# The last up projection of a two-layer encoder by Strassen's scheme, with the gated chunks kept in DRAM

## The chip, the cores and the metric

The kernel runs on one core of one Trainium2 chip. Its time is the device time of one execution in microseconds (us), the median of several runs. TensorE does the matrix products, VectorE (DVE in the profile) and ScalarE (ACT) everything that is done per element, GpSimd (POOL) a few small operations, and SyncE's queue (SP) starts the transfers.

## What is computed

The input is 1024 tokens of 1024 numbers. Two layers follow one another; each has a token mixer (sparse attention in layer 0, retention in layer 1) and then a gated feed-forward part with a short causal convolution. The change is in the feed-forward part of the last layer:

```python
def conv_ffn(h, w_up, conv_w, conv_b, w_down):
    seq = h.shape[1]
    u = h @ w_up                                   # (1024, 1024) @ (1024, 5632)
    up = jnp.pad(u, ((0, 0), (CONV_W - 1, 0), (0, 0)))
    u = sum(up[:, j:j + seq] * conv_w[j] for j in range(CONV_W)) + conv_b
    a, b = u[..., :D_FF], u[..., D_FF:]            # D_FF = 2816 = 22 chunks of 128
    return (jax.nn.silu(a) * b) @ w_down

x = x + conv_ffn(rms_norm(x, norm_ffn_g[i]), f_w_up[i], f_conv_w[i], f_conv_b[i], f_w_down[i])
```

## The kernel before

Channels lie on the 128 partitions and tokens along the rows; the 1024 tokens are two halves of 512, and `x[0]`, `x[1]` hold the running sum of each half as 8 chunks of 128 channels. Every product of two float32 matrices is made of three: each operand is split into a high part `hi` (a ScalarE copy to a narrower format) and a rest `lo` (a VectorE subtraction), and `mm3` (L134 to L136) adds hi times hi, hi times lo and lo times hi in one bank of PSUM, the accumulator memory. There are 8 banks of 128 x 512 numbers.

Weights come through a queue. `wprep` loads one block of 128 x 1024 into `wraw` (2 buffers), splits it into `whi` (L98) and `wlo` (L100; 3 buffers each), and `weight` keeps two blocks ahead of the one in use.

The last stage is `ffn` in mode `FULL`, over both halves at once. For each of the 22 chunks `c` it makes four projections (`proj_T`, 24 matmuls each: chunk `c` and chunk `22 + c` of the weights, for each half); `conv` takes each bank, multiplies it by the tokens' 1/rms (L552), and applies the three taps (L556 to L558; the last two columns of the first half are kept in `halo` for the second); then SiLU (L576), the product with the other side (L578) and the split into `ghf`, `glf` (L580, L581). After every fourth chunk the down projection of that group follows, 8 blocks of weights for both halves, each result added to `x` (L593). The normalised input `hh`, `hl` of a half is `x` times a gain, split (L145, L146); 1/rms is applied afterwards. For the first half this is done inside the second half's retention (`early` in `retention`), for the second half behind it.

The order in which each engine's instructions stand is made by a planner when the program is built, from the order of the code and what each instruction waits for. On the chip every engine keeps its order: an instruction that waits holds up all that stand behind it on its engine, the issue of transfers on SP's queue too.

## Time and profile before

| | |
|---|---|
| median of 3 runs | 2853.04 us (2852.39 to 2853.21) |
| span of the profiled execution, first to last instruction | 2850.1 us |
| TensorE busy | 2755.8 us, 97% of the span |
| VectorE busy | 1823.4 us, 64% |
| ScalarE busy | 1049.9 us, 37% |
| last stage (up and down projection of layer 1) | about from 2112 to the end |

The span leaves out what lies before the first and after the last instruction. Busy time counts an instruction from start to end, so matmuls that overlap in the pipeline are better counted by the distance of their starts.

### The profile page before, as it was taken

What the parts mean: (1) busy time and instruction counts of PE and PEld (TensorE: products, weight loads), DVE (VectorE), ACT (ScalarE), POOL (GpSimd) and SP (SyncE); (2) the same over time, 40 slices, a digit from 0 to 9 for tenths busy, and PEclk for the clock granted to TensorE, in tenths of its full rate; (3) what the DMA queues carried; (4) which work ended last, traced back from release to release, by engine and by line L of the source; (5) the groups of instructions that cost most, each with busy time, mean ns of one, the idle gap of its engine ahead of it and who ended that gap; (6) DMA issues with size and microseconds to landing.
All of it is one profiled execution on the core that took longest, in us unless ns stands there. A gap on an engine that the chain in (4) does not pass through costs nothing.

```text
span 2850.1 us, 32404 instructions
## 1 busy us (share of the span) xinstructions
PE 2755.8 (97%) x12416; PEld 2263.7 (79%) x12416; DVE 1823.4 (64%) x3180; ACT 1049.9 (37%) x1588; POOL 379.1 (13%) x247
## 2 busy tenths in 40 slices
PE   8978998998999999999999999999999999999999
PEld 6756786776787888888888888888888888888887
DVE  5798899997685454455766764444556564656464
ACT  6437433332473333334433443233343232323231
POOL 2554334344430000000000000000000000000000
PEclk9988999999999999999999999999999999999999
DMA  5220123222211222232233232222221111111112
GB/s 193 76 87 32 60 74 94 70 96 74 82 38 67 82 96 74 81 104 74 91 102 96 91 102 97 82 75 95 87 69 45 52 41 56 37 60 34 63 37 90
DMA packets 72763, 217.76 MB, mean 76 GB/s; under 512 B 8224, under 2 KB 10656, under 8 KB 72608
## 3 DMA queue, kind: packets, MB, share of 16 engines
q1 hardware_dynamic: 72608, 215.70, 23.2%
q8 instruction: 97, 1.59, 0.2%
q14 instruction: 58, 0.48, 0.1%
HBM read 205.71 MB, written 6.29 MB: 74 GB/s over the span
## 4 chain that ended last, share of the span: by engine, by line
PE 74%; DVE 11%; issue 1%; ACT 1%; POOL 0%; DMA 0%; POOLq 0%; ACTq 0%; DVEq 0%
PE bank L134 24%; PE bank L136 24%; PE bank L135 24%; DVE scratch L417 4%; DVE t L558 2%; DVE t L557 1%; DVE t L552 1%; PE bank L526 1%; DVE gl L581 1%; DVE x L593 0%; PE bank L759 0%; POOL wlo L100 0%; DVE tkb L427 0%; DVE t L578 0%; ACT hh L145 0%
## 5 line engine op out<-in xcount | busy, mean ns | idle before, releaser
L134 PE MATMUL bank<-hh,whi 128*128 128x512 f32 (+2 forms) x1888 | 738.2, 391 | 16.9 <-ACT hh L145 10.6
L136 PE MATMUL bank<-hh,wlo 128*128 128x512 f32 (+2 forms) x1888 | 736.5, 390 | 10.4 <-POOL wlo L100 10.4
L135 PE MATMUL bank<-hl,whi 128*128 128x512 f32 (+2 forms) x1888 | 735.7, 390 | 3.5 <-DVE hl L146 3.4
L98 ACT ACTIVATE whi<-wraw 128x1024 fp32r<-128x1024 f32 (+4 forms) x416 | 400.0, 962 | 887.9 <-PE bank L135 607.3
L100 DVE TENSOR_TENSOR wlo<-wraw,whi 128x1024 fp32r<-128x1024 f32 (+4 forms) x319 | 350.9, 1101 | 306.8 <-ACT whi L98 303.5
L134 PEld LDWEIGHTS bank<-hh,whi 128*128 128x128 f32 (+1 forms) x1888 | 356.3, 189 | 93.8 <-ACT hh L145 12.3
L136 PEld LDWEIGHTS bank<-hh,wlo 128*128 128x128 f32 (+1 forms) x1888 | 356.1, 189 | 90.3 <-POOL wlo L100 15.1
L135 PEld LDWEIGHTS bank<-hl,whi 128*128 128x128 f32 (+1 forms) x1888 | 356.1, 189 | 79.1 <-DVE hl L146 4.3
L100 POOL TENSOR_TENSOR wlo<-wraw,whi 128x1024 fp32r<-128x1024 f32 (+2 forms) x97 | 219.8, 2268 | 308.9 <-ACT whi L98 293.4
L552 DVE TENSOR_TENSOR t<-bank,rbc 128x512 f32<-128x512 f32 x176 | 120.9, 688 | 169.7 <-PE bank L136 168.4
L556 ACT ACTIVATE t<-t,cols 128x512 f32<-128x512 f32 x176 | 142.5, 813 | 229.8 <-DVE t L552 228.9
L593 DVE TENSOR_TENSOR x<-x,bank 128x512 f32<-128x512 f32 x160 | 109.2, 685 | 181.8 <-PE bank L136 181.4
L135 PE MATMUL bank<-wlo,hh 128*128 128x512 f32 x512 | 199.3, 389 | 0.0
L136 PE MATMUL bank<-whi,hl 128*128 128x512 f32 x512 | 199.2, 389 | 0.0
L134 PE MATMUL bank<-whi,hh 128*128 128x512 f32 x512 | 198.8, 390 | 0.0
L417 DVE TENSOR_SCALAR_CACHE_REDUCE scratch<-sc,tkt 128x640 f16<-128x640 f32 (+1 forms) x192 | 180.5, 940 | 1.9
L558 DVE SCALAR_TENSOR_TENSOR t<-t,cols,t 128x510 f32<-128x510 f32 x176 | 155.9, 886 | 3.8
L136 PE MATMUL bank<-gh,wlo 128*128 128x512 f32 x352 | 139.9, 399 | 14.3 <-POOL wlo L100 14.0
L557 DVE SCALAR_TENSOR_TENSOR t<-t,cols,t 128x511 f32<-128x511 f32 x176 | 142.1, 807 | 11.4 <-ACT t L556 8.6
L134 PE MATMUL bank<-gh,whi 128*128 128x512 f32 x352 | 138.7, 396 | 5.6 <-ACT whi L98 5.6
L135 PE MATMUL bank<-gl,whi 128*128 128x512 f32 x352 | 138.6, 394 | 0.0
L135 PE MATMUL bank<-glf,whi 128*128 128x512 f32 x352 | 136.8, 389 | 0.0
(213 smaller groups left out, 4189.7 us busy)
## 6 DMA issues: line engine op xcount, KB each, us to landing
wraw<-in_wf_up SPq DMA_DIRECT2D x132, 512.0 KB, 3.2
wraw<-in_wb_vg SPq DMA_DIRECT2D x64, 512.0 KB, 3.2
wraw<-in_wf_dn SPq DMA_DIRECT2D x48, 384.0 KB, 3.1
wraw<-in_wb_qk SPq DMA_DIRECT2D x32, 512.0 KB, 3.2
wraw<-in_wb_out SPq DMA_DIRECT2D x32, 512.0 KB, 3.2
wraw<-in_wf_dn SPq DMA_DIRECT2D x56, 256.0 KB, 2.7
wraw<-in_wa_in SPq DMA_DIRECT2D x26, 512.0 KB, 3.4
x<-in_xT SPq DMA_DIRECT2D x16, 512.0 KB, 7.3
```

The lines of the kernel that those rows point to most:

```text
L98: nc.scalar.activation(hi[:, :n], raw[:, :n], AF.Copy)
L100: eng.tensor_tensor(lo[:, :n], raw[:, :n], hi[:, :n].bitcast(F32), ALU.subtract)
L134: mm(ps, ah, bh, start=first, stop=False)
L135: mm(ps, ah, bl, start=False, stop=False)
L136: mm(ps, al, bh, start=False, stop=last)
L417: V.tensor_scalar(scratch[:, 0, :Ls[b]], scs[b], of(b), None, op0=op, op1=ALU.add, accum_out=cnt[:, b:b + 1])
L526: nc.tensor.transpose(pt[:, i * 128:(i + 1) * 128], lg[:, i, j * 128:(j + 1) * 128], self.ident)
L552: nc.vector.tensor_tensor(pn, ps, rbc, ALU.mult)
L556: nc.scalar.activation(u, ps, AF.Identity, bias=w(3), scale=w(2))
L557: nc.vector.scalar_tensor_tensor(u[:, 1:], ps[:, :511], w(1), u[:, 1:], op0=ALU.mult, op1=ALU.add)
L558: nc.vector.scalar_tensor_tensor(u[:, 2:], ps[:, :510], w(0), u[:, 2:], op0=ALU.mult, op1=ALU.add)
L593: nc.vector.tensor_tensor(x[:, m], x[:, m], ps, ALU.add)
```

## The change

Up to the second half's retention both programs issue the same instructions in the same order. Then the last `ffn` is replaced by `ffn_whole`. It takes the product of two blocks of weight outputs (chunk `c`, chunk `22 + c`) by two halves of the input channels with two halves of the channels by two halves of the tokens, a product of 2 by 2 blocks, with 7 block products for 8 (`product`, 12 matmuls each). In exchange there are sums of weight blocks (`t3`, `a21`, `a11`, `a12` in `prep_b`), sums of input blocks made once (`T1` to `T4`), and sums of results (the `add` calls behind the products). Inputs are now normalised in place beforehand (`normaliser`), so `x` is first written to DRAM (`xd`) and read back at the end. The results of both halves lie side by side (`ca`, `cb`, 1024 wide), so the convolution runs once over 1024 columns. SiLU of one side (`ud[0]`) and the other side (`ud[1]`) are written to DRAM. When all 22 chunks are through, a separate loop reads them, multiplies and splits them (`gate`) and makes the down projection in four groups instead of six. The first block products of the first `PRE` = 4 chunks (`first`: those that need only the first half of the tokens) are issued ahead, the first of them inside the retention.

```diff
...
 HALF = ([(0, 6), (6, 6), (12, 6), (18, 4)], 8, 2)
-FULL = ([(0, 4), (4, 4), (8, 4), (12, 4), (16, 4), (20, 2)], 5, 1)
+DOWN = [(0, 6), (6, 6), (12, 6), (18, 4)]
+PRE = 4
...
-    def retention(self, half, x, early):
+    def retention(self, half, x, then=None, early=lambda: None):
...
                 early()
+            if n in (1, 3) and then:
+                next(then)
             for j in range(4):
...
                 nxt = qk_proj(n + 1)
+            elif then:
+                next(then)
             y = self.ogp.tile([128, 2, 4, 512], F32R, tag="og", name="y")
...
                         self.square_sum(x, m)
+                        nc.sync.dma_start(self.xd[half][m], x[:, m])
+    def split(self, hi, lo, raw):
+        return (self.nc.scalar.activation(hi, raw, AF.Copy),
+                self.nc.vector.tensor_tensor(lo, raw, hi.bitcast(F32), ALU.subtract))
+    def normaliser(self, x, gc, half):
+        rbc = self.tp.tile([128, 512], F32, tag="rbc", bufs=1, name="rbc")
+        self.nc.scalar.activation(rbc, self.bcast(self.tok[half][1], range(4)), AF.Copy)
+        def chunk(k):
+            self.nc.vector.scalar_tensor_tensor(x[:, k], x[:, k], self.col(gc + k), rbc, op0=ALU.mult, op1=ALU.mult)
+        return chunk
...
+    def product(self, ps, w, t, first, last):
+        for k in range(4):
+            a, b = w[0][:, k * 128:(k + 1) * 128], w[1][:, k * 128:(k + 1) * 128]
+            for i, (u, v) in enumerate(((a, t[:, 0, k]), (a, t[:, 1, k]), (b, t[:, 0, k]))):
+                self.nc.tensor.matmul(ps, u, v, start=first and k + i == 0, stop=k == 3 and i == 2,
+                                      skip_group_check=not (first and last))
+    def ffn_whole(self, l, x):
+        nc = self.nc
+        add = lambda o, a, b, op=ALU.add: nc.vector.tensor_tensor(o, a, b, op)
+        x0, x1 = x
...
+        def prep_a(c):
+            raw = load(c)
+            return raw, halves(raw)
+        def prep_b(c, raw):
+            rb = load(NFF + c)
+            a11, a12, a21, a22 = raw[:, :512], raw[:, 512:], rb[:, :512], rb[:, 512:]
+            t3 = s3.tile([128, 512], F32, tag="t3", name="t3")
+            add(t3, a11, a21, ALU.subtract)
+            add(a21, a21, a22)
+            s1, a22 = halves(rb)
+            add(a11, rb[:, :512], a11, ALU.subtract)
+            add(a12, a12, a11, ALU.subtract)
+            s2, s4 = halves(raw)
+            return s1, s2, halves(t3, s3, 512, "3")[0], s4, a22
+        def first(wa, keep=None):
+            a, e = self.bank(), self.bank()
+            self.product(a, wa[0], B11, True, False)
+            p1 = self.tmp()
+            nc.scalar.activation(p1, a, AF.Copy)
+            self.product(e, wa[1], B21, True, True)
+            if keep is None:
+                keep = self.tmp()
+            add(keep, e, p1)
+            return a, keep
+        chunk = self.normaliser(x0, gc, 0)
+        for k in range(8):
+            chunk(k)
+        yield
+        B11, B21 = [self.hp.tile([128, 2, 4, 512], F32R, tag="h", name=n) for n in ("B11", "B21")]
+        for t, o in ((B11, 0), (B21, 4)):
+            for k in (0, 2):
+                self.split(two(t, 0, k), two(t, 1, k), two(x0, o + k))
+        wa = [prep_a(0)]
+        yield
+        pre = [first(wa[0][1])]
+        tt, s3 = yield
+        T = lambda name: tt.tile([128, 2, 4, 512], F32R, tag="T", name=name)
+        wa += [prep_a(c) for c in range(1, PRE)]
+        pre.append(first(wa[1][1]))
+        self.mean_square(1)
+        pre.append(first(wa[2][1]))
+        chunk = self.normaliser(x1, gc, 1)
+        pre += [first(w) for _, w in wa[3:]]
+        nxt = prep_b(0, wa[0][0])
+        T1, T2, T4, B22, T3 = [T(n) for n in ("T1", "T2", "T4", "B22", "T3")]
+        for k in (0, 2):
+            chunk(k)
+            chunk(k + 1)
+            add(two(x0, k), two(x1, k), two(x0, k), ALU.subtract)
+            self.split(two(T1, 0, k), two(T1, 1, k), two(x0, k))
+        for k in range(4):
+            chunk(4 + k)
+            t2 = self.tmp()
+            add(t2, x1[:, 4 + k], x0[:, k], ALU.subtract)
+            self.split(T2[:, 0, k], T2[:, 1, k], t2)
+            add(x0[:, 4 + k], x0[:, 4 + k], t2, ALU.subtract)
+        for k in (0, 2):
+            self.split(two(T4, 0, k), two(T4, 1, k), two(x0, 4 + k))
+        for k in (0, 2):
+            self.split(two(B22, 0, k), two(B22, 1, k), two(x1, 4 + k))
+        for k in (0, 2):
+            add(two(x1, k), two(x1, 4 + k), two(x1, k), ALU.subtract)
+            self.split(two(T3, 0, k), two(T3, 1, k), two(x1, k))
+        cu = [self.xp.tile([128, 4, 1024], F32, tag="x", name="cu") for _ in range(2)]
+        def conv(ct, u, c):
+            w = lambda j: self.col(C_CONV + (l * 44 + c) * 4 + j)
+            nc.scalar.activation(u, ct, AF.Identity, bias=w(3), scale=w(2))
+            nc.vector.scalar_tensor_tensor(u[:, 1:], ct[:, :1023], w(1), u[:, 1:], op0=ALU.mult, op1=ALU.add)
+            nc.vector.scalar_tensor_tensor(u[:, 2:], ct[:, :1022], w(0), u[:, 2:], op0=ALU.mult, op1=ALU.add)
+        for c in range(NFF):
+            s1, s2, s3_, s4, a22 = nxt
+            ca, cb, ua, ub = (cu[c % 2][:, i] for i in range(4))
+            if pre:
+                a, c11 = pre.pop(0)
+                nc.scalar.activation(ca[:, :512], c11, AF.Copy)
+            else:
+                a, _ = first(wn, ca[:, :512])
+            d = self.bank()
+            self.product(d, s1, T1, True, False)
+            p5 = self.tmp()
+            nc.scalar.activation(p5, d, AF.Copy)
+            self.product(a, s2, T2, False, False)
+            u2 = self.tmp()
+            nc.scalar.activation(u2, a, AF.Copy)
+            f = self.bank()
+            self.product(f, a22, T4, True, True)
+            p4 = self.tmp()
+            nc.scalar.activation(p4, f, AF.Copy)
+            self.product(d, s4, B22, False, True)
+            add(ca[:, 512:], d, u2)
+            self.product(a, s3_, T3, False, True)
+            add(cb[:, :512], a, p4)
+            add(cb[:, 512:], a, p5)
+            if c + 1 < NFF:
+                raw, wn = prep_a(c + 1) if c + 1 >= PRE else (load(c + 1), None)
+                nxt = prep_b(c + 1, raw)
+            conv(ca, ua, c)
+            nc.scalar.activation(ua, ua, AF.Silu)
+            nc.sync.dma_start(self.ud[0][c], ua)
+            conv(cb, ub, NFF + c)
+            nc.sync.dma_start(self.ud[1][c], ub)
+        todo = [(g0, n, m) for g0, n in DOWN for m in range(8)]
+        ready = []
+        def dn(i):
...
+        buf = self.hp.tile([128, 4, 1024], F32, tag="h", name="gin")
+        gates = {}
+        def gate(c):
+            ga, gb = buf[:, c % 2 * 2], buf[:, c % 2 * 2 + 1]
+            nc.sync.dma_start(ga, self.ud[0][c])
+            nc.sync.dma_start(gb, self.ud[1][c])
+            add(ga, ga, gb, ALU.mult)
+            if c % 2 == 0:
+                p, tag = (self.hp, "h") if c in (0, 12) else (tt, "T")
+                self.gt = p.tile([128, 2, 2, 1024], F32R, tag=tag, name="g")
+            g = self.gt[:, c % 2]
+            self.split(g[:, 0], g[:, 1], ga)
+            gates[c] = g
+        dn(0)
+        gate(0)
+        dn(1)
+        for c in range(1, DOWN[0][1]):
+            gate(c)
+        y = [self.xp.tile([128, 8, 512], F32, tag="x", name="xo") for _ in range(2)]
+        for m in range(8):
+            for h in range(2):
+                nc.sync.dma_start(y[h][:, m], self.xd[h][m])
+        for i, (g0, n, m) in enumerate(todo):
+            if i + 2 < len(todo):
+                dn(i + 2)
+            if m == 2 and g0 + n < NFF:
+                ahead = list(range(g0 + n, min(g0 + n + DOWN[0][1], NFF)))
+            if m >= 2 and g0 + n < NFF and ahead:
+                gate(ahead.pop(0))
+            hi, lo = ready[i]
+            for h in range(2):
+                ps = self.bank()
+                for k in range(n):
+                    g = gates[g0 + k]
+                    sl = slice(h * 512, (h + 1) * 512)
+                    self.mm3(ps, hi[:, k * 128:(k + 1) * 128], lo[:, k * 128:(k + 1) * 128], g[:, 0, sl], g[:, 1, sl],
+                             k == 0, k == n - 1)
+                add(y[h][:, m], y[h][:, m], ps)
+                if g0 + n == NFF:
+                    nc.sync.dma_start(self.out[m * 128:(m + 1) * 128, h * H:(h + 1) * H], y[h][:, m])
     def run(self):
...
         self.plan_weights([("inproj", 0), ("inproj", 1), ("outproj", 0), ("ffn", (0, HALF, True)), ("outproj", 1),
-                           ("ret", 0), ("ffn", (0, HALF, False)), ("ret", 1), ("ffn", (1, FULL, False))])
+                           ("ret", 0), ("ffn", (0, HALF, False)), ("ret", 1)])
...
-            self.ogp = pool("og", 2)
+            inner = es.enter_context(ExitStack())
+            self.ogp = inner.enter_context(tc.tile_pool(name="og", bufs=2, reuse_waits="tile"))
...
+            self.xd = [[dp.tile([128, 512], F32, name=f"xd{h}_{m}") for m in range(8)] for h in range(2)]
+            self.ud = [[dp.tile([128, 1024], F32, name=f"ud{i}_{c}") for c in range(NFF)] for i in range(2)]
...
                 self.later(1, lambda: self.mean_square(1))
-                self.retention(0, x[0], lambda: parts.append(self.ffn_part(0, 1, x[1])))
+                self.retention(0, x[0], None, lambda: parts.append(self.ffn_part(0, 1, x[1])))
...
                 self.later(1, lambda: self.mean_square(1))
-                self.retention(1, x[1], lambda: parts.append(self.ffn_part(1, 0, x[0])))
-            with tc.tile_pool(name="ring", bufs=1, reuse_waits="tile") as rp:
-                og = (self.ogp, "og")
-                self.later(2, lambda: self.mean_square(1))
-                parts.append(self.ffn_part(1, 1, x[1], (og, og), rp, lag=4))
-                R = FULL[1]
-                gh = rp.tile([128, R, 2, 512], F32R, name="ghf")
-                gl = rp.tile([128, R, 2, 512], F32R, name="glf")
-                self.ffn(1, FULL, parts, lambda c, i: (gh[:, c % R, i], gl[:, c % R, i]), last=True)
+                last = self.ffn_whole(1, x)
+                self.retention(1, x[1], last)
+            inner.close()
+            with tc.tile_pool(name="T", bufs=5, reuse_waits="tile") as tt, \
+                    tc.tile_pool(name="s3", bufs=1, reuse_waits="tile") as s3:
+                for _ in iter(lambda: last.send((tt, s3)), None):
+                    pass
...
```

Three places show how the order moves. In `t2_...`, `bank_...` and the like the number tells buffers apart.

The first place is VectorE where the last stage begins. Before, it splits the second half's input (`hl`) and goes straight to the first chunk's convolution:

```order
L146 SCALAR_TENSOR_TENSOR hl_16435<-x_7351,cols_84,hh_16434 128x512 x7
L100 TENSOR_TENSOR wlo_16457<-wraw_16455,whi_16456 128x1024
L185 TENSOR_TENSOR acc_16291<-acc_16291,t2_16427 128x512
L146 SCALAR_TENSOR_TENSOR hl_16435<-x_7351,cols_84,hh_16434 128x512
L552 TENSOR_TENSOR t2_16588<-bank_16467,rbc_16151 128x512
L561 COPY halo_91<-t2_16588 128x2
L557 SCALAR_TENSOR_TENSOR t2_16590<-t2_16588,cols_84,t2_16590 128x511
L558 SCALAR_TENSOR_TENSOR t2_16590<-t2_16588,cols_84,t2_16590 128x510
L194 TENSOR_SCALAR msq_16528<-bank_16523 128x4
L100 TENSOR_TENSOR wlo_16463<-wraw_16461,whi_16462 128x1024
```

Now the eight chunks are first normalised in place (L795); then come the sums and splits of the input blocks (L821 and L787 on `x`, `t2`, `T1` to `T4`, `B22`), among those of the weights (`wraw`) and one sum of a result (`bank`), before any convolution:

```order
L795 SCALAR_TENSOR_TENSOR x_7411<-x_7411,cols_84,rbc_16631 128x512 x8
L821 TENSOR_TENSOR x_2809<-x_7411,x_2809 128x1024
L821 TENSOR_TENSOR t3_16818<-wraw_16814,wraw_16816 128x512
L821 TENSOR_TENSOR x_2809<-x_7411,x_2809 128x1024
L821 TENSOR_TENSOR t2_16666<-bank_16639,t2_16652 128x512
L821 TENSOR_TENSOR t2_16703<-x_7411,x_2809 128x512
L821 TENSOR_TENSOR t2_16709<-x_7411,x_2809 128x512
L821 TENSOR_TENSOR x_7411<-x_7411 128x1024
L821 TENSOR_TENSOR wraw_16816<-wraw_16816 128x512
L787 TENSOR_TENSOR T1_16687<-x_2809,T1_16687 128x1024
L821 TENSOR_TENSOR x_7411<-x_7411 128x1024
L821 TENSOR_TENSOR t2_16715<-x_7411,x_2809 128x512
```

These are the first 12 of 31 rows, 39 instructions in all, down to the split of the second chunk's weights; the convolution begins two rows later.

The second place is VectorE in the middle of the up projection. Before, it works on one chunk half by half, in pieces of 512 columns:

```order
L552 TENSOR_TENSOR t2_16888<-bank_16788,rbc_16151 128x512
L561 COPY halo_91<-t2_16888 128x2
L581 TENSOR_TENSOR glf_16454<-t2_16767,ghf_16453 128x512
L557 SCALAR_TENSOR_TENSOR t2_16890<-t2_16888,cols_84,t2_16890 128x511
L558 SCALAR_TENSOR_TENSOR t2_16890<-t2_16888,cols_84,t2_16890 128x510
L100 TENSOR_TENSOR wlo_16784<-wraw_16782,whi_16783 128x1024
L552 TENSOR_TENSOR t2_16896<-bank_16838,rbc_16151 128x512
L561 COPY halo_91<-t2_16896 128x2
L552 TENSOR_TENSOR t2_16906<-bank_16813,rbc_16452 128x512
L557 SCALAR_TENSOR_TENSOR t2_16898<-t2_16896,cols_84,t2_16898 128x511
```

Now one chunk is 17 instructions; these are 12 of them (L911 and L912 are the convolution, L821 on `bank` takes a result out of PSUM, L787 is a split); two sums of results, a split of 512 and two pieces of convolution make up the rest:

```order
L821 TENSOR_TENSOR t3_17664<-wraw_17656,wraw_17662 128x512
L911 SCALAR_TENSOR_TENSOR cu_16740<-cu_16740,cols_84 128x1023
L821 TENSOR_TENSOR wraw_17662<-wraw_17662 128x512
L821 TENSOR_TENSOR cu_16741<-bank_17557,t2_17570 128x512
L912 SCALAR_TENSOR_TENSOR cu_16740<-cu_16740,cols_84 128x1022
L787 TENSOR_TENSOR wlo_17659<-wraw_17656,whi_17658 128x1024
L821 TENSOR_TENSOR wraw_17656<-wraw_17662,wraw_17656 128x512
L821 TENSOR_TENSOR wraw_17656<-wraw_17656 128x512
L787 TENSOR_TENSOR wlo_17668<-wraw_17662,whi_17667 128x1024
L821 TENSOR_TENSOR cu_16741<-bank_17585,t2_17612 128x512
L787 TENSOR_TENSOR wlo_17674<-wraw_17656,whi_17673 128x1024
L911 SCALAR_TENSOR_TENSOR cu_16741<-cu_16741,cols_84 128x1023
```

The weights that are summed and split here are those of the next chunk, between the results of this one.

The third place is TensorE where the down projection begins. Before, a group of it stood directly behind a chunk's up projection:

```order
L135 MATMUL bank_17163<-hl_16435,whi_16933 128x512
L136 MATMUL bank_17163<-hh_16434,wlo_16934 128x512
L134 MATMUL bank_17232<-ghf_16453,whi_17077 128x512
L135 MATMUL bank_17232<-glf_16454,whi_17077 128x512
L136 MATMUL bank_17232<-ghf_16453,wlo_17078 128x512
L134 MATMUL bank_17232<-ghf_16453,whi_17077 128x512
```

Now it is behind the last chunk; `g_19551` holds the gated chunks 0 and 1, `g_19568` chunks 2 and 3, and six banks stand open at once, so that each gated chunk is used for three blocks of weights before the next one is wanted:

```order
L137 MATMUL bank_19729<-g_19551,whi_19607 128x512
L138 MATMUL bank_19729<-g_19551,whi_19607 128x512
L139 MATMUL bank_19729<-g_19551,wlo_19608 128x512
L137 MATMUL bank_19611<-g_19568,whi_19544 128x512
L137 MATMUL bank_19631<-g_19568,whi_19544 128x512
L137 MATMUL bank_19657<-g_19568,whi_19556 128x512
L137 MATMUL bank_19677<-g_19568,whi_19556 128x512
L137 MATMUL bank_19709<-g_19568,whi_19607 128x512
L137 MATMUL bank_19729<-g_19551,whi_19607 128x512
```

## Rows read from the trace of the kernel before

**Rows 1.** the page's busy times: us, share of the span, instructions

```profile
PE 2755.8 (97%) x12416; PEld 2263.7 (79%) x12416; DVE 1823.4 (64%) x3180; ACT 1049.9 (37%) x1588; POOL 379.1 (13%) x247
```

**Rows 2.** busy time of each engine in a stretch of the last stage

```profile
core 0: us, PE busy (x) PEld busy (x) DVE busy (x) ACT busy (x) POOL busy (x), PEclk, DMA share, GB/s
2200.00:2300.00 100.00, 100.00 (x443) 82.84 (x442) 50.47 (x82) 24.52 (x33) 0.00 (x0) 1.00 0.16 51
```

**Rows 3.** waits of TensorE from 2050 to the end: total us, times, longest

```profile
PE bank L759 <- DVE sg L734: 1.1, 1, 1.1
PE bank L134 <- ACT y L145: 0.5, 1, 0.5
```

**Rows 4.** timeline of TensorE: start us, us, what; 25 matmuls apart

```profile
2079.94 0.39 PE L134 MATMUL bank<-whi,hh 128*128 128x512 f32 x1
...
2085.61 0.39 PE L135 MATMUL bank<-wlo,hh 128*128 128x512 f32 x1
```

**Rows 5.** groups by line and shape, 2100 to the end: busy us, mean ns

```profile
L134 PE MATMUL bank<-hh,whi 128*128 128x512 f32 x704 | 274.1, 389 | 0.0
...
L134 PE MATMUL bank<-ghf,whi 128*128 128x512 f32 x352 | 136.3, 389 | 0.0
...
L556 ACT ACTIVATE t<-t,cols 128x512 f32<-128x512 f32 x88 | 71.2, 815 | 161.4 <-DVE t L552 161.4
...
L558 DVE SCALAR_TENSOR_TENSOR t<-t,cols,t 128x510 f32<-128x510 f32 x88 | 65.8, 748 | 2.1
L557 DVE SCALAR_TENSOR_TENSOR t<-t,cols,t 128x511 f32<-128x511 f32 x88 | 65.8, 748 | 8.9 <-ACT t L556 6.1
L593 DVE TENSOR_TENSOR x<-x,bank 128x512 f32<-128x512 f32 x96 | 65.7, 687 | 114.7 <-PE bank L136 114.4
...
L100 DVE TENSOR_TENSOR wlo<-wraw,whi 128x1024 fp32r<-128x1024 f32 x45 | 55.1, 1224 | 51.1 <-ACT whi L98 50.0 <-PE bank L156 1.1
L98 ACT ACTIVATE whi<-wraw 128x1024 fp32r<-128x1024 f32 x45 | 47.8, 1061 | 86.9 <-PE bank L135 86.6 <-ACT hh L145 0.3
L578 DVE TENSOR_TENSOR t<-t,t 128x512 f32<-128x512 f32 x44 | 30.3, 689 | 2.2
...
L576 ACT ACTIVATE t<-t 128x512 f32<-128x512 f32 x44 | 27.8, 633 | 39.0 <-DVE t L558 36.4 <-DVE t L564 2.6
...
L602 ACT ACTIVATE rbc<-bank 128x512 f32<-128x512 f32 x2 | 1.2, 598 | 4.4 <-PE bank L156 4.3
```

**Rows 6.** timeline of VectorE: start us, us of work without a gap, what, count

```profile
2114.29 1.22 DVE L100 TENSOR_TENSOR wlo<-wraw,whi 128x1024 fp32r<-128x1024 f32 x1
2115.43 0.68 DVE L185 TENSOR_TENSOR acc<-acc,t 128x512 f32<-128x512 f32 x1
...
2126.08 4.72 DVE L146 SCALAR_TENSOR_TENSOR hl<-x,cols,hh 128x512 fp32r<-128x512 f32 x7
...
2829.10 1.28 DVE L593 TENSOR_TENSOR x<-x,bank 128x512 f32<-128x512 f32 x2
```

**Rows 7.** DMA issues: count, KB each, median us from issue to landing

```profile
wraw<-in_wf_up SPq DMA_DIRECT2D x132, 512.0 KB, 3.2
...
x<-in_xT SPq DMA_DIRECT2D x16, 512.0 KB, 7.3
```

**Rows 8.** TensorE busy us, granted clock, DMA share and GB/s in three stretches

```profile
10.00:20.00 10.00, 10.00 (x40) 1.00 1.04 383
...
350.00:360.00 10.00, 5.37 (x16) 0.52 0.15 52
360.00:370.00 10.00, 10.00 (x48) 0.97 0.16 55
```

**Rows 9.** the end: timeline of TensorE, then of VectorE

```profile
2845.93 0.39 PE L136 MATMUL bank<-ghf,wlo 128*128 128x512 f32 x1
...
2846.36 0.69 DVE L593 TENSOR_TENSOR x<-x,bank 128x512 f32<-128x512 f32 x1 [0.67 <-PE bank L136]
```

23 lines of the change are left out of this document (added).

## The prediction

> **What bounds the kernel now.** I read the page's busy times first: TensorE is at work for 97% of the span, VectorE for 64% [rows 1]. A share over the whole span says nothing of one stage, so I went to a stretch of the last stage: TensorE busy all the time, at full clock (1.00, its 2.4 GHz level), VectorE for half of it and ScalarE for a quarter [rows 2]. The waits of TensorE from 2050 to the end are two, 1.6 us together, both before the last output projection of the retention [rows 3]. So from 2112 on TensorE never waits, and only fewer or faster matmuls can shorten this stage. The distance of starts gives the price of one: 25 matmuls in 5.67 us, 0.2268 us each [rows 4]; the 389 ns of the groups is the length of one in the pipeline [rows 5].
>
> **What is removed.** An up projection of 22 chunks took 22 x 4 x 24 = 2112 matmuls; now it takes 22 x 7 x 12 = 1848. The down projection keeps its 1056. 264 matmuls x 0.2268 = 59.9 us less. The new ones are of the same shape, each with its own weight load as before, so I take the same price.
>
> **Does VectorE keep up in the up projection?** One chunk now occupies TensorE for 84 x 0.2268 = 19.05 us. VectorE's 17 instructions a chunk: three splits of 1024 columns (1.224 us alone [rows 5], 1.14 from start to start when they follow one another [rows 6]); nine operations of 512 columns (0.69 alone, 0.60 in a row: two in 1.28 [rows 5, 6]); four convolution pieces of 1023 columns. No row has these; from 748 ns for 511 [rows 5] and 1.224 less 0.689 us for 512 more columns [rows 5] I estimate 1.28 alone and 1.20 in a row. In a row that is 3.4 + 5.4 + 4.8 = 13.6 us, alone 3.7 + 6.2 + 5.1 = 15.0. Both are below 19.05. ScalarE has 3 x 1.06 and 0.63 for splits, four copies out of PSUM of 0.60, two scalings (0.815 for 512, so 1.24 for 1024, an estimate from the same slope) and a SiLU of about 1.06 [rows 5]: 9.8 us. I also followed the order through one chunk: TensorE reads the two weight buffers that the next chunk needs until 13.6 and 16.3 us of the chunk, so their splits end at 15.9 and 18.6; the next chunk wants them at 5.4 and 8.2 us of its own 19.05. The raw block that follows is loaded from 18.7 on, lands 3.2 us later [rows 7], and VectorE asks for it some 0.8 us after that. About 4 us of a chunk stay free on VectorE. I take no wait in chunks 4 to 21; a miss of 0.5 us a chunk would be 9 us.
>
> **The new stall: the start.** Let 0 be the end of the retention's last matmul. TensorE has three `first` calls left, 72 matmuls, 16.3 us, and about 1 us of small ones: 17.3. The mean square stands behind the first of these calls and the broadcast of 1/rms behind the second: 5.4 + 0.5 + 5.4 + 0.5 = 11.8. Its copy on ScalarE stands behind a weight split (1.06) and takes 0.60, so VectorE can begin to normalise the second half at about 13.5. The 39 instructions that then stand on VectorE ahead of the first convolution are 8 of the kind of L146 (4.72 for seven, 0.67 each [rows 6]), 14 of 1024 columns and 17 of 512: 5.4 + 16.0 + 10.2 = 31.6 us, to 45. The first split for `T1` can be made at 20.7, so TensorE stands from 17.3 to 20.8, and then gets blocks as they come: `T1` complete at 29, `B22` at 39, `T2` and `T4` only at 42 to 44. Chunks 0 and 1 need 120 matmuls, 27.2 us, and would end at 44.5 without waits. Following the order, at 46.5 (the copy of the sum after `T2`) there are still 47 of them to run (`T3` of chunk 0; `T2`, `B22`, `T3` of chunk 1): end at 57.2, 12.7 us lost. Chunk 2 then waits another 1.9 for its weight sums, since VectorE has the results of chunk 0 and 1 before them. Together 14.6 us. If every operation costs what it does alone (31.6 becomes 34.8) and chunks 1 to 3, which take TensorE only 13.6 us each, go at 15.0 and pay again for what VectorE is behind, it is 22; if the splits need not wait for the copy and for weight buffers, 9.
>
> **TensorE's clock in that stall.** Where TensorE was busy for 5.37 of 10 us, the granted clock was 0.52, and 0.97 in the ten after [rows 8]. The stretch from 17 to 57 will be about 70% busy in pieces. I add 2 us (about half of 10 us of work at the lower level, less what waits anyway); the ends are 0 and 8. *TensorE: Matmul & The Clock Gate* in the Trainium skill, section "HAM oscillation — how this bites in real kernels", says that idle gaps put the array back to half clock and that each burst after such a gap starts slow. By that rule all 120 matmuls of chunks 0 and 1 would run at twice the distance, and the sum would be up to 18 us higher; the rows agree that the clock falls, and show it back after one stretch.
>
> **The new seam before the down projection.** The first six gated chunks must be read back (two of 512 KB each), multiplied and split. The buffers of `first` fall free 2.7 us into the last chunk. Along VectorE's order (multiply and split 1.2 each, ScalarE's 1.06 between, two buffers, a load of 3.2) I get chunk 1 at 14, 2 at 24, 3 at 28, 4 at 33 and 5 at 36 us after the last chunk's start. TensorE comes there at 19; with six banks open it asks for them at 19, 28, 31, 37 and 41. So 4 to 7 us are to spare, and I take 1 us; if pairs of loads land like those that queue at the kernel's start (7.3 [rows 7]), up to 8. Later groups need 6 reads in 65 us of matmuls: hidden. The reads, 23 MB and 4 MB of `x`, come with the weights to at most 250 GB/s in the first 80 us; the kernel has moved 383 [rows 8].
>
> **The rest.** The two waits of [rows 3] are covered by the first `first`, which stands there now: -1.1, between 0 and -1.6. The 8 normalisations of the first half inside the retention (5.4 us of VectorE at the second head) lie behind a projection of 21.8 us: 0, at most 2. The tail is the same: last matmul, sum, store [rows 9]. GpSimd and the stages before are unchanged: 0.
>
> **The sum.** -59.9 + 14.6 + 2 + 1 - 1.1 = -43.4. The span of 2850.1 becomes 2806.7; the runs' median lies 2.9 above the span, so 2853.04 becomes 2809.6, about 2810. The small ends, 9 + 0 + 0 - 1.6, give 2800.5; the large ones, 22 + 8 + 8 + 0, give 2831.
>
> **Rivals.** (1) The start costs more: VectorE at its lone prices and the clock low to the end of chunk 3, 22 + 8 or more in place of 16.6: 2820 to 2836. For it: VectorE is the only engine with work there and order is kept. (2) The start is nearly hidden, 5 us in place of 16.6: 2798. Against it: 1/rms cannot be there before 12. (3) The down projection starves: its reads are chained through two buffers and stand in SP's queue among weight loads. At 8 us for the seam and 3 for each of the three later groups, 2826; at 10 a group, 2847, no gain that can be told. Against it: [rows 8]. (4) Slower than before: the chain through the raw buffer sets the chunk. Split, load, sums, split again is some 12 us of VectorE and ScalarE plus a load of 3.2, 15.3 us. It decides from a load of about 7 us (19.05 less 12), and eats the whole gain when 18 chunks last 43.4 / 18 = 2.4 us longer, at a load of 9.5. With loads of 11 us a chunk takes 23: 2810 + 18 x 4 = 2882. For it: two stores of 512 KB a chunk now stand ahead of the loads in SP's queue, and loads that queued took 7.3 [rows 7]. Against it: the queue moves some 2 MB in 19 us, 110 GB/s.
>
> **How the numbers follow.** The forecast (2800 to 2820) has 0.58, rival 1 0.17, rival 2 0.08, rival 3 0.06 (0.05 faster, 0.01 the same), rival 4 0.11 (0.04 within 0.2%, 0.07 slower). About 0.2% (5.7 us) is what a measurement of this kernel can tell from no change. That makes 0.88 faster, 0.05 the same, 0.07 slower. The range 2798 to 2832 takes in the forecast, most of rival 1 and part of the second and third.
>
> **What would show it.** TensorE should go through chunks 4 to 21 without idle time at 19.05 us each, VectorE busy for 70 to 80% there; the waits of the new product line should lie in the 60 us after the retention, some 15 us, with VectorE's splits (L787) as what ended them; the down projection should take 1056 x 0.2268 = 239.5 us from its first matmul. I am wrong if the product line waits in every chunk, if loads of `wraw` take over 7 us, or if the granted clock stays low behind the start.

## The result, and the profile after

The changed kernel takes 2806.30 us (median of 4 runs, 2805.32 to 2808.24), the kernel before 2852.72 us (4 runs, 2852.23 to 2853.21): a ratio of 0.9838, with a 95% interval of 0.9824 to 0.9852. Forecast were 2810 us and a range of 2798 to 2832. The profiled execution has a span of 2806.4 us, 43.7 less than the 2850.1 of before; the sum said 43.4 less. (The medians lie 46.4 apart: the profiled execution was the slowest of the four, 2808.24 us.) That the spans agree to 0.3 us is in part luck, since the same instructions up to the last stage take some us more in one profile than in another (see the end).

TensorE still is the engine at work all the time, and issues 264 matmuls less than in [rows 1]. The first line is the page's list of busy times (share of the span, instructions); the last three are from its list of transfers (count, KB each, median us to landing):

```profile
PE 2697.8 (96%) x12152; PEld 2211.7 (79%) x12152; DVE 1872.5 (67%) x3028; ACT 1110.8 (40%) x1620; POOL 379.7 (14%) x247
...
wraw<-in_wf_up SPq DMA_DIRECT2D x135, 512.0 KB, 3.3
...
ud<-cu SPq DMA_DIRECT2D x44, 512.0 KB, 2.6
gin<-ud SPq DMA_DIRECT2D x44, 512.0 KB, 4.7
```

The waits of TensorE from 2050 us to the end (total us, times, longest), which answer [rows 3]: both waits of before are gone (0.3 us is left, on `y`), and the product line L809 waits four times, 10.4 us together, for `T` blocks made by ScalarE and VectorE.

```profile
PE bank L809 <- ACT T L786: 8.0, 2, 6.3
PE bank L809 <- DVE T L787: 2.4, 2, 2.0
PE bank L137 <- ACT g L786: 0.3, 1, 0.3
PE bank L138 <- DVE y L149: 0.3, 1, 0.3
PE bank L137 <- ACT whi L786: 0.2, 1, 0.2
```

Where they lie shows TensorE's timeline (start, length, engine, line, names, idle time before it). The last `y` matmul, the retention's last, starts at 2130.78, so the prediction's point 0 is 2131.01, where the next one starts. After the 72 matmuls of `first`, TensorE stands from 2149.35 to 2155.62, gets single matmuls, and waits for the last time at 2178.39; the down projection begins at 2561.89:

```profile
2130.78 0.39 PE L139 MATMUL bank<-y,wlo 128*128 128x512 f32 x1
...
2148.96 0.39 PE L809 MATMUL bank<-B,wlo 128*128 128x512 f32 x1
2155.62 0.80 PE L809 MATMUL bank<-T,whi 128*128 128x512 f32 x1 [6.27 <-ACT T L786]
2158.14 0.79 PE L809 MATMUL bank<-T,whi 128*128 128x512 f32 x1 [1.72 <-ACT T L786]
2160.95 0.79 PE L809 MATMUL bank<-T,whi 128*128 128x512 f32 x1 [2.02 <-DVE T L787]
2161.54 0.63 PE L809 MATMUL bank<-T,wlo 128*128 128x512 f32 x1
2161.97 1.05 PE L809 MATMUL bank<-T,whi 128*128 128x512 f32 x2
...
2178.39 0.50 PE L809 MATMUL bank<-T,whi 128*128 128x512 f32 x1 [0.40 <-DVE T L787]
...
2561.89 0.39 PE L137 MATMUL bank<-g,whi 128*128 128x512 f32 x1
...
2802.20 0.39 PE L139 MATMUL bank<-g,wlo 128*128 128x512 f32 x1
```

The windows of that start and of the steady part (stretch and its length, then busy us and instruction count of PE, PEld, DVE, ACT and POOL, granted clock, DMA share, GB/s). In the start VectorE is at work all the time while TensorE stands; later it is the other way round, TensorE busy for all of 100 us with the 443 matmuls of [rows 2], VectorE at 75%:

```profile
2151.01:2161.01 10.00, 1.65 (x3) 0.64 (x3) 10.00 (x14) 4.40 (x5) 0.00 (x0) 0.58 0.01 4
2161.01:2171.01 10.00, 10.00 (x32) 7.61 (x33) 10.00 (x14) 6.48 (x8) 0.00 (x0) 0.74 0.17 52
...
2300.00:2400.00 100.00, 100.00 (x443) 82.81 (x442) 75.00 (x86) 49.07 (x58) 0.00 (x0) 1.00 0.31 114
...
2560.00:2580.00 20.00, 19.66 (x88) 15.93 (x87) 14.61 (x15) 6.74 (x6) 0.00 (x0) 1.00 0.98 373
```

**The balance**, from the end of the retention's last matmul to the start of the last one of all. The retention ends before with

```profile
2125.05 0.39 PE L136 MATMUL bank<-y,wlo 128*128 128x512 f32 x1
```

So it is 720.65 us before (2125.28 to 2845.93). After: the 24 matmuls of the first `first`, which now stand ahead of point 0 (5.44), then 430.88 up to the down projection, then 240.31 to the last matmul, 676.63 in all: 44.0 less. What lies ahead is 0.3 longer and the tail the same (4.20 for 4.17 us). The 1824 matmuls of the 430.88 us are 413.7, 16 small ones 1.6: so the start lost **15.6 us**, all but 0.2 of it up to 2178.39: the 1690 matmuls from there to 2561.89 take 383.5 us, and their price is 383.3. Of the 15.6, 10.4 are waits; the rest is matmuls that came one at a time or ran slowly behind a wait.

### The profile page after: what moved, and what is told of

The parts are those of the page before. It is cut to its first block, busy times and chain, and to the rows that moved or that the text cites. A ratio compares the mean times of both kernels' runs of the same rounds, so it can differ in the third digit from the quotient of the medians.

```text
span 2806.4 us, 31988 instructions
## 1 busy us (share of the span) xinstructions
PE 2697.8 (96%) x12152; PEld 2211.7 (79%) x12152; DVE 1872.5 (67%) x3028; ACT 1110.8 (40%) x1620; POOL 379.7 (14%) x247
## 4 chain that ended last, share of the span: by engine, by line
PE 71%; DVE 9%; issue 2%; DMA 2%; POOL 1%; ACT 1%; SPq 0%; POOLq 0%; ACTq 0%; DVEq 0%
PE bank L137 19%; PE bank L139 19%; PE bank L138 19%; PE bank L809 13%; DVE scratch L420 3%; POOL wlo L103 1%; DVE t L561 1%; DMA gin<-ud 1%; DVE t L560 1%; PE bank L529 1%; DMA wraw<-in_wf_up 1%; DVE t L555 1%; DVE gl L584 0%; PE bank L766 0%; DMA wraw<-in_wf_dn 0%
## 5 line engine op out<-in xcount | busy, mean ns | idle before, releaser
L101 ACT ACTIVATE whi<-wraw 128x1024 fp32r<-128x1024 f32 (+3 forms) x324 | 324.5, 1003 | 676.6 <-PE bank L138 392.7
L137 PE MATMUL bank<-hh,whi 128*128 128x512 f32 (+2 forms) x1184 | 464.9, 393 | 17.9 <-ACT hh L148 11.6
L139 PE MATMUL bank<-hh,wlo 128*128 128x512 f32 (+2 forms) x1184 | 462.2, 391 | 11.0 <-POOL wlo L103 11.0
L138 PE MATMUL bank<-hl,whi 128*128 128x512 f32 (+2 forms) x1184 | 461.5, 390 | 3.5 <-DVE hl L149 3.4
L103 DVE TENSOR_TENSOR wlo<-wraw,whi 128x1024 fp32r<-128x1024 f32 (+3 forms) x227 | 266.6, 1175 | 240.8 <-ACT whi L101 238.0
L139 PEld LDWEIGHTS bank<-hh,wlo 128*128 128x128 f32 (+1 forms) x1184 | 224.0, 189 | 63.9 <-POOL wlo L103 16.1
L809 PE MATMUL bank<-T,whi 128*128 128x512 f32 x704 | 220.0, 394 | 10.4 <-ACT T L786 8.0
L786 ACT ACTIVATE whi<-wraw 128x1024 fp32r<-128x1024 f32 (+2 forms) x98 | 95.4, 973 | 198.7 <-PE bank L138 127.5
L809 PEld LDWEIGHTS bank<-T,whi 128*128 128x128 f32 x704 | 133.3, 189 | 41.2 <-ACT T L786 9.3
L809 PE MATMUL bank<-B,whi 128*128 128x512 f32 x528 | 162.8, 389 | 0.0
L787 DVE TENSOR_TENSOR wlo<-wraw,whi 128x1024 fp32r<-128x1024 f32 (+2 forms) x98 | 109.1, 1113 | 75.5 <-ACT whi L786 75.4
L809 PE MATMUL bank<-T,wlo 128*128 128x512 f32 x352 | 137.5, 392 | 0.0
```

The source lines that it names most:

```text
L101: nc.scalar.activation(hi[:, :n], raw[:, :n], AF.Copy)
L103: eng.tensor_tensor(lo[:, :n], raw[:, :n], hi[:, :n].bitcast(F32), ALU.subtract)
L137: mm(ps, ah, bh, start=first, stop=False)
L138: mm(ps, ah, bl, start=False, stop=False)
L139: mm(ps, al, bh, start=False, stop=last)
L786: return (self.nc.scalar.activation(hi, raw, AF.Copy), self.nc.vector.tensor_tensor(lo, raw, hi.bitcast(F32), ALU.subtract))
```

## Experiments

For small differences I read two stretches off each trace: **up**, from point 0 (end of the last `y` matmul) to the first matmul of the down projection, and **down**, from there to the last matmul. They are 430.88 and 240.31 us in the changed kernel. They leave out the part before the retention's end, in which profiles of the same instructions differ by up to 4.7 us (see the end).

**Eight products in the same frame.** Only the scheme is undone; DRAM, normalised inputs and the separate down projection stay:

```diff
-            self.product(d, s1, T1, True, False)
...
-            add(cb[:, 512:], a, p5)
+            nc.scalar.activation(ca[:, :512], pre.pop(0) if pre else first(wa), AF.Copy)
+            nc.scalar.activation(cb[:, :512], first(wb), AF.Copy)
+            nc.scalar.activation(cb[:, 512:], first(wb, (B12, B22)), AF.Copy)
+            nc.scalar.activation(ca[:, 512:], first(wa, (B12, B22)), AF.Copy)
```

> The same frame (inputs normalised beforehand, gated chunks through DRAM, separate down projection, first projections of four chunks ahead) with 8 plain block products of 12 matmuls instead of 7, so without any sums: 3168 matmuls again. Theory (the gain is the price of 264 matmuls less the stall at the start, the frame costs nothing): 2852.7 of before, +1.6 for 16 more small matmuls, +1 in the down projection, -1.3 for the two waits, 0 to 4 for a shorter start (only eight normalisations and four splits before the second half can be used): 2854, 2850 to 2860. Rival (the frame itself costs, by transfers or by the seam, and the products gave more than 60): above 2864. Rival (the frame itself gives part of the gain): below 2847.

Measured: 2850.37 us against 2852.91 of before, ratio 0.9991 (0.9982 to 1.0001). Up took 475.15 us, and its 2088 matmuls and 16 small ones are 475.2: nothing is lost at all. The ends of up, and TensorE's waits from 2080 to the end, which are one row:

```profile
2128.26 0.39 PE L139 MATMUL bank<-y,wlo 128*128 128x512 f32 x1
...
2603.64 0.39 PE L137 MATMUL bank<-g,whi 128*128 128x512 f32 x1
```
```profile
PE bank L137 <- ACT y L148: 0.2, 1, 0.2
```

From the retention's last matmul to the last one of all it is 5.44 + 475.15 + 239.13 = 719.7 us, for 720.65 before. So the frame costs nothing and gives nothing that can be told, and the whole gain is that of seven products: 475.15 - 430.88 = 44.3 us, which is 59.9 less the 15.6 of the start. (The expectation's 16 more small matmuls are none: the pages of both kernels count 12416 matmuls in all.)

**One product more in each chunk from the fifth on.**

```diff
             self.product(f, a22, T4, True, True)
+            if c >= PRE:
+                self.product(f, a22, T4, False, True)
```

> From chunk 4 on one of the seven products (second weight row block by T4) is issued twice into the same bank, so its part counts double in the result: 18 x 12 = 216 matmuls more. Theory (TensorE sets the pace of every chunk, no other engine does): 2806 + 216 x 0.2268 = 2806 + 49.0 = 2855. Rival (VectorE or the raw buffers set the pace in part of the time): an added matmul is partly hidden, at half 2831, at most hidden 2806.

Measured: 2853.9 us; up 479.42, so 48.5 us for 216 matmuls, 0.225 us each, in a run whose last wait of the start came 0.4 us earlier; with that it is 0.2267. The price of [rows 4] holds for the new products, and nothing of it is hidden.

**Three products less in each chunk from the fifth on** (the sums and splits for them stay).

```diff
-            self.product(a, s2, T2, False, False)
+            if c < PRE:
+                self.product(a, s2, T2, False, False)
```
(and the same for the products with `B22` and `T3`)

> From chunk 4 on three of the seven products are left out (those with T2, B22 and T3), while all of their splits and sums are still made; TensorE has 48 matmuls a chunk, 10.9 us. Theory (VectorE comes next, with 14.1 us of work in a chunk of 19.05 as the trace shows, at most 15.3 with the raw buffers' chain): 18 x (14.1 to 15.3 less 19.05) = -89 to -68, so 2717 to 2738. Rival (the raw buffer chain is longer than I followed it and is nearly the bound already): over 17 us a chunk, above 2770. Rival (nothing but TensorE): 18 x -8.17, 2659.

Measured: 2757.4 us, 19 above the upper end, but only part of that is the chunks. Up took 368.6 us, 62.3 less: 3.5 a chunk, so some 15.6 us a chunk and not 14.1 to 15.3. (The last 2.67 us of up are a wait for the down projection's input.) Down took 250.07 us, 9.8 more, which the expectation did not have, and point 0 lies 1.7 us later. The ends of up and down, a window of 100 us, the waits of TensorE from 2250 to 2500, and two rows of ScalarE's timeline:

```profile
2132.47 0.39 PE L139 MATMUL bank<-y,wlo 128*128 128x512 f32 x1
...
2501.30 0.50 PE L137 MATMUL bank<-g,whi 128*128 128x512 f32 x1 [2.67 <-ACT g L786]
...
2751.37 0.39 PE L139 MATMUL bank<-g,wlo 128*128 128x512 f32 x1
```
```profile
2300.00:2400.00 100.00, 78.97 (x298) 60.24 (x296) 88.01 (x104) 57.61 (x69) 0.00 (x0) 0.90 0.37 130
```
```profile
PE bank L809 <- DVE wlo L787: 30.6, 15, 3.0
PE bank L809 <- ACT whi L786: 17.9, 9, 2.7
```
```profile
2357.80 1.06 ACT L786 ACTIVATE whi<-wraw 128x1024 fp32r<-128x1024 f32 x1 [2.74 <-DMA wraw<-in_wf_up]
...
2370.87 1.06 ACT L786 ACTIVATE whi<-wraw 128x1024 fp32r<-128x1024 f32 x1 [3.61 <-DVE wraw L821]
```

TensorE now waits for weight blocks, yet VectorE is at work for 88%, not 100%. ScalarE's splits of these blocks wait for a load here and for VectorE's sums there: so, as I read these rows, the chain of rival 4 (split, load, sums, split through two raw buffers) sets the pace, a little ahead of VectorE's sum of work; the prediction gave it 15.3 us. A chunk has some 3.5 us to spare against it. (The granted clock was 0.90 there, so part of TensorE's own work is longer too.)

**Weight loads two and three times over.**

```diff
-            nc.sync.dma_start(raw, up[l, c])
+            for _ in range(3 if PRE < c % NFF else 1):
+                nc.sync.dma_start(raw, up[l, c])
```
(and with 2 for 3)

> In chunks 5 to 21 each raw weight block is loaded three times over, one load after the other, before it is used. Loads of the two blocks are then done some 7 to 10 us later than in the trace (3.3 us for each further load, part of them side by side). Theory (a delay up to the 4.1 to 4.9 us that VectorE is idle in a chunk is hidden, what goes beyond it is paid in each of 17 chunks): 17 x (2.5 to 5.5) = +43 to +93, 2849 to 2899. Rival (loads are hidden behind TensorE whatever they take): under 2815. Rival (there is no reserve, the chain sets the chunk already): 17 x 7 or more, above 2925.

Measured: 2884.2 us, 78 more, of which up has 67.9, 4.0 in each of the 17 chunks, and down 6.5: within what was expected. VectorE's timeline in one chunk shows the chain stretched, ScalarE's split late behind the load, and VectorE behind the split:

```profile
2376.95 1.23 DVE L787 TENSOR_TENSOR wlo<-wraw,whi 128x1024 fp32r<-128x1024 f32 x1 [9.17 <-ACT whi L786]
2378.10 0.68 DVE L821 TENSOR_TENSOR cu<-bank,t 128x512 f32<-128x512 f32 x1
2381.79 0.69 DVE L821 TENSOR_TENSOR t<-wraw 128x512 f32<-128x512 f32 x1 [3.01 <-DMA wraw<-in_wf_up]
```

> In chunks 5 to 21 each raw weight block is loaded twice over. In the order that is built the second block of a chunk then lands some 4.1 us later than in the trace (11.25 + 3 x 3.3 + 0.3 against two loads side by side). If the reserve of a chunk is the 4.1 to 4.9 us that VectorE is idle in the trace: nothing is paid, 2806 to 2810. If it is the 2.7 us that the run with three products left out showed (16.3 us a chunk), and that the run with threefold loads agrees with (4.6 paid of some 7.4 of delay): 17 x 1.4, 2830. Rival (the delay is paid in full): 17 x 4.1, 2876.

Measured: 2807.1 us, up 430.47: nothing. The figure of 2830 was wrong: it rested on a reserve of 2.7 us, for which I had divided the whole difference of the run above among the chunks, the longer down projection with it (and so 4.6 for 4.0 a chunk in the run with threefold loads). VectorE came to the loaded blocks 10.6 us after its split of the chunk (2330.50 to 2341.14) for 5.3 in the changed kernel (2331.76 to 2337.09), and waited only 1.0 us, since the planner had put the convolution of the chunk ahead:

```profile
2341.14 0.69 DVE L821 TENSOR_TENSOR t<-wraw 128x512 f32<-128x512 f32 x1 [0.98 <-DMA wraw<-in_wf_up]
```

So rival 4 is real, and far off: with each block loaded twice, so that VectorE uses it some 5 us later, nothing is paid; with each loaded three times, more than the whole gain.

**The start: the late weight block.** VectorE's timeline in the changed kernel:

```profile
2141.83 0.69 DVE L821 TENSOR_TENSOR t<-wraw 128x512 f32<-128x512 f32 x1 [2.67 <-DMA wraw<-in_wf_up]
...
2147.96 5.38 DVE L795 SCALAR_TENSOR_TENSOR x<-x,cols,rbc 128x512 f32<-128x512 f32 x8
...
2177.12 1.22 DVE L787 TENSOR_TENSOR T<-x,T 128x1024 fp32r<-128x1024 f32 x1
```

It waits for the second weight block of chunk 0, which was the fourth load through one raw buffer (the other holds the first block), and the normalisation stands behind that. The edit gives this block memory that `T3` takes later:

```diff
+        rb0 = tt.tile([128, 4, 1024], F32, tag="T", name="r0")[:, 0]
+        nc.sync.dma_start(rb0, up[l, NFF])
...
-        nxt = prep_b(0, wa[0][0])
+        nxt = prep_b(0, wa[0][0], rb0)
```

> The second weight block of chunk 0 is loaded into a buffer of its own (the memory that T3 takes later) instead of the second raw slot, where it was fourth in line and landed 10.8 us after the retention's last matmul. Theory A (that load holds up VectorE and, through the order on ScalarE, the normalisation: it began at 17.0, not at the 13.5 of the prediction): normalisation begins 3 to 4 us earlier, TensorE's first wait shrinks from 6.3 to about 3 us, 2803. Theory B (1/rms or VectorE's list of 39 instructions sets the stall, the load only fills a gap): 2806, same waits.

Measured: up 428.04, 2.84 less. The normalisation began at 14.1 after point 0 instead of 17.0, TensorE's first wait is 2.88 instead of 6.27, and its last wait comes 2.84 us earlier after point 0 (2177.59 less 2133.05, for 47.38):

```profile
2154.82 0.51 PE L809 MATMUL bank<-T,whi 128*128 128x512 f32 x1 [2.88 <-ACT T L786]
...
2177.59 0.50 PE L809 MATMUL bank<-T,whi 128*128 128x512 f32 x1 [0.40 <-DVE T L787]
```

Theory A holds in the trace; but the median is 2806.04 (2804.66 to 2807.48), 0.3 less. So it was run again:

> The run with the own buffer for the second block of chunk 0 once more, in more rounds. Its stretch from the retention's last matmul to the down projection was 2.8 us shorter than that of the changed kernel, its median only 0.3 us lower; the traces show the retention's last matmul anywhere from 2128.3 to 2133.1 us in kernels that are the same up to there. If that scatter hid the gain: a median of 2803 to 2804.5. If the early part of this build is later as a rule, by what the edit gave: 2806 again, and the stretch again 428.

Measured: 2805.55 us (2804.63 to 2807.14), ratio to before 0.9836 (0.9823 to 0.9850); up 428.09; point 0 at 2133.20 for 2133.05 the first time and 2131.01 in the changed kernel. That is nearer the second case: in both profiled executions the part up to the retention's end took some 2 us more than in the one of the changed kernel, and what the edit wins afterwards can't be told from the kernels' times. Whether those 2 us belong to the build isn't shown, as the changed kernel was profiled once.

**The start: five chunks ahead.** `PRE = 5` for 4, alone and with the edit above.

> First block products of five chunks ahead instead of four: TensorE has 24 matmuls (5.4 us) more before it needs the second half of the tokens; in the built order the normalisation now stands ahead of the weight sums of chunk 0. Theory A (the stall is TensorE standing empty at 18 us while VectorE prepares): the 6.3 us of the first wait are filled, the granted clock stays up, 5 to 10 us less, 2796 to 2801. Theory B (VectorE's work through the first chunks sets the end of the start; what is issued ahead only moves the wait to later chunks): 2806 within 2, with new waits at chunks 1 to 4.

> Both edits together: own buffer for the second block of chunk 0, and five chunks ahead. Theory A: no wait at the first T block, 10 us of the waits and most of the clock's loss gone, 2793 to 2799. Theory B: 2804 to 2806.

Measured: 2809.4 us (up 433.08) and 2807.4 us (up 430.94). Theory A was wrong, and both runs are slower than Theory B had them too: the 5.4 us of work are there when TensorE would have stood empty, but new waits come behind. With `PRE = 5` alone:

```profile
2163.05 0.80 PE L809 MATMUL bank<-T,wlo 128*128 128x512 f32 x1 [3.57 <-DVE wlo L787]
...
2176.44 1.44 PE L809 MATMUL bank<-T,whi 128*128 128x512 f32 x2 [4.47 <-ACT T L786]
```

What decides is the last wait, how many matmuls the trace still has from there to the down projection, and how fast they run. In the changed kernel the last wait ends 47.4 us after point 0 with 1690 matmuls left, with the own buffer at 44.5 with 1690, with five ahead at 44.5 with 1703, with both at 46.1 with 1690. In the first two these take what the price of 0.2268 says, within 0.2 us. With five ahead they take 388.5 us (433.08 less 44.53), 2.3 more than their price of 386.2: TensorE has stood for 4.47 us just before, and the clock granted in the 5 us behind is 0.51, its lower level (1.2 GHz), and 1.00 in the next 5:

```profile
2176.44:2181.44 5.00, 5.00 (x11) 3.75 (x12) 5.00 (x7) 3.40 (x5) 0.00 (x0) 0.51 0.00 0
2181.44:2186.44 5.00, 5.00 (x23) 4.13 (x22) 3.27 (x4) 2.75 (x3) 0.00 (x0) 1.00 0.33 111
```

With both edits it is 1.5 more than the price. So what TensorE loses before its last wait is without price, and work put there saves only what it takes from behind it; but a long wait at the end is paid once more in slow matmuls behind it.

**The start: GpSimd helps.** GpSimd makes the low parts of `T4` and `B22`.

```diff
-            self.split(two(B22, 0, k), two(B22, 1, k), two(x1, 4 + k))
+            nc.scalar.activation(two(B22, 0, k), two(x1, 4 + k), AF.Copy)
+            nc.gpsimd.tensor_tensor(two(B22, 1, k), two(x1, 4 + k), two(B22, 0, k).bitcast(F32), ALU.subtract)
```
(and the same for `T4`)

> As the run with both edits, and GpSimd makes the low parts of T4 and B22 (four subtractions of 1024 columns, 2.3 us each as its splits in layer 0 take) that VectorE made at 1.14 us. Theory A (VectorE's list is what is late now): VectorE is 4.6 us shorter, up to 4 us less than with both edits alone. Theory B (nothing waits for VectorE any more, or GpSimd's 2.3 us each make T4 and B22 later): the same within 1 us, or 1 to 3 us more.

Measured: 2809.9 us, up 433.55, 2.6 more than without it, as Theory B had it. TensorE's longest wait is 4.8 us on GpSimd's `T`. GpSimd's timeline:

```profile
2168.73 9.85 POOL L902 TENSOR_TENSOR T<-x,T 128x1024 fp32r<-128x1024 f32 x1 [24.68 <-ACT T L901]
2178.55 4.70 POOL L905 TENSOR_TENSOR B<-x,B 128x1024 fp32r<-128x1024 f32 x2
```

**The start: without the normalisation.**

```diff
         for k in (0, 2):
-            chunk(k)
-            chunk(k + 1)
             add(two(x0, k), two(x1, k), two(x0, k), ALU.subtract)
...
-            chunk(4 + k)
```

> As the run with the own buffer for the second block of chunk 0, but the eight multiplications that normalise the second half of the tokens are left out (its inputs are then not divided by their rms), and with them the wait for 1/rms. To be read from the retention's last matmul to the first matmul of the down projection, which was 428.0 us there (1824 matmuls are 413.7). Theory (VectorE's queue sets the end of the start: 5.4 us of work and 2.9 us of idle time fall away): 420 to 423, waits of 1 to 4 us left. Rival (TensorE waits for something other than VectorE's queue, weight blocks or banks): 426 or more.

Measured: up 430.09 (2807.3 us). My theory fell and the rival holds: the last `T` block was ready at 2168.7, 37.6 us after point 0, and yet up is 2.0 us longer than with the own buffer alone. The waits moved to weight blocks:

```profile
2157.73 0.79 PE L809 MATMUL bank<-T,whi 128*128 128x512 f32 x1 [3.58 <-DVE T L787]
2186.62 1.71 PE L809 MATMUL bank<-T,whi 128*128 128x512 f32 x4 [1.80 <-ACT whi L786]
2190.35 1.22 PE L809 MATMUL bank<-T,whi 128*128 128x512 f32 x2 [2.02 <-ACT whi L786]
```

At the last of them, 59.3 us after point 0, the trace has 1628 matmuls left, four less than chunks 2 to 21 have (1632): TensorE waits for the weight sums of chunk 2, which stand on VectorE among the results of chunks 0 and 1. The 1628 take 1.6 us more than their price (granted clock 0.65 in the 5 us from 2190.35). With the own buffer alone TensorE comes to 1628 left at 58.6. So there are two chains of nearly the same length at the start, that of the `T` blocks and that of chunk 2's weights: shortening the first by 2.8 us shortened up as much, and with the first much shorter the second set the end. The planner's order differs between these runs, so how far the second is behind in the changed kernel itself isn't shown.

**The start: 1/rms earlier.** On top of the own buffer, the broadcast of 1/rms in the middle of the third `first`, and chunk 3's block in the spare memory too.

```diff
+            if mid:
+                mid()
             self.product(e, wa[1], B21, True, True)
...
+        pre.append(first(wa[2][1], mid=lambda: norm.append(self.normaliser(x1, gc, 1))))
```

> On top of the own buffer for the second block of chunk 0, the weight block of chunk 3 is loaded into that same spare memory, and the broadcast of 1/rms stands in the middle of the third first product instead of behind it. Theory (VectorE's queue): 1/rms can be used 2 to 3 us earlier, and since VectorE is idle for only 2.9 us in the 14 us before it, the stretch from the retention's last matmul to the down projection falls from 428.0 to 425 to 427; the median, 2806.0 there, to about 2804. Rival (1/rms alone gates it): to 422 to 424. Rival (VectorE's work is all that counts and only its order changes): 428.

Measured: 2813.3 us (ratio to before 0.9861, 0.9845 to 0.9877), up 437.18, 9 more than without it: none of the three cases. The broadcast waited itself, in front of the product behind it, and in the planner's new order chunk 2's weights came still later. (Which of the two edits did that isn't separated.)

```profile
2143.34 1.85 PE L159 MATMUL bank<-kon,rms 128*128 128x128 f32 x8 [2.15 <-POOL rms L153]
...
2194.81 1.19 PE L809 MATMUL bank<-T,whi 128*128 128x512 f32 x4 [1.80 <-ACT whi L786]
2198.55 1.22 PE L809 MATMUL bank<-T,whi 128*128 128x512 f32 x2 [2.54 <-ACT whi L786]
```

No version ran faster than the changed kernel by more than the runs can tell. A version that makes chunk 2's weight sums earlier as well wasn't tried.

## Why the prediction was right, step by step

- **Fewer matmuls, -59.9.** Right: 0.225 to 0.227 us each by the run with one product more, and 44.3 + 15.6 = 59.9 by the run with eight.
- **VectorE keeps up.** Right: ScalarE's `SiLU` comes every 19.05 us (2318.22, 2337.27), no wait from the start's end to the down projection, VectorE 71 to 81% busy in the windows of 100 us. The estimates of 1.28 us for a convolution piece and 1.24 for a scaling were measured at 1.28 and 1.23 to 1.25. The reserve of "about 4 us" was some 3.5 against TensorE going faster; blocks that were used some 5 us later cost nothing.
- **The start, 14.6.** 15.6 us were lost. The mechanism held, but the sum is nearer than its parts, by luck: two of them were too small and one too large. That VectorE "can begin to normalise the second half at about 13.5" failed: it began at 17.0, because I had followed the chain of 1/rms but not the raw buffer's, through which the second block of chunk 0 came fourth. The run with its own buffer shows what that was worth, 2.84. The list of 39 instructions took 32.0 us (2147.96 to 2180.0) for the 31.6 of the sum. The last wait ended at 47.4 for 46.5, and 58 matmuls of chunks 0 and 1 were left then, not 47 (1690 less 1632): 0.9 and 2.5 us more. On the other side, the 1.9 us for chunk 2 did not come: behind the later `T` blocks its weights were in time. It is there, though, as the chain that took over in the run without normalisation. The waits of the product line were 10.4 us, not "some 15", and ScalarE's splits (L786) ended 8.0 of them, which stand behind VectorE's sums; VectorE's splits (L787), which were to end them, ended 2.4.
- **The clock, 2 (0 to 8).** It cost nothing that can be seen. It did fall: 0.58 and 0.74 of the 2.4 GHz level in the two windows above, and the first matmuls after the gap are 0.8 us long and some 0.43 apart; from about 2166.4 on they are 0.227 apart again. *TensorE: Matmul & The Clock Gate* in the Trainium skill, section "HAM oscillation — how this bites in real kernels", says that a burst behind an idle gap starts slow, and the trace agrees; the 18 us that the rule would have made of it did not come. TensorE waited once more at 2178.39 for VectorE, which had worked without a gap since 2141.83, so what TensorE had lost until then would have been waiting otherwise. Where the last wait itself was long, as with `PRE = 5`, the low clock behind it cost 2.3 us. That is read from the traces; no run changed the clock alone.
- **The seam, 1 (0 to 8).** Down took 240.31 us, 1.0 more than 1055 x 0.2268. But the "4 to 7 us" that I had to spare were none: TensorE waited 0.34 for `g` and 0.19 for a weight block, and the reads issued until 2600 landed in 6.1 us (median, 3.3 to 8.3), not 3.2. The queue moved 352 GB/s from 2550 to 2600 and 314 in the 80 us from 2550, not "at most 250". Where TensorE came to it earlier against VectorE's work, or the last blocks later, the seam cost 11 and 8 us: down is 250.1 with three products left out and 246.8 with threefold loads. So the mechanism of rival 3 was nearer than its chance of 0.06 says.
- **The two waits, -1.1.** -1.3. The small matmuls (mean square and broadcast, 0.1 us each) are as many as before: 24 behind the retention's last matmul before, 16 now, the other 8 inside the retention. So it was right to have none in the sum.
- **The bottom line.** 2809.6 came from the span's 2806.7 plus 2.9; the span was 2806.4, and the median lay 0.1 below it, since the profiled execution was a late one.

## What to carry to other kernels

A product scheme that saves matmuls gains their price as long as the engines that make the sums end before TensorE in each block; an added product and a few left out measure both sides of that in two runs. At the joint between two stages look for TensorE's last wait and for what is left to run behind it: gaps and a low clock ahead of it are free, and filling them gains nothing unless that wait moves; a long gap at that wait is paid again in slow matmuls behind it. When a chain there is shortened, ask which one comes next: here 2.8 us could be won at the first, and then the next was near. And when a run's time is divided among its blocks, take the stretch in which they lie: with three products left out the down projection behind them had become longer too.
